# Stick-breaking triangle sums: one fp32 matmul against two fp32r matmuls on high part and remainder

## The chip, the cores and the metric

One core of a Trainium2 chip runs the whole layer as one program. The metric is the device time of one execution in microseconds; shown is the median of three runs, and beside it one execution that was profiled.

## What is computed

One layer of a streaming encoder on x of 256 x 2048 (float32): a SwiGLU block (hidden width 5632) with a layer norm, a mixer with two branches (mLSTM with 4 heads of 256, stick-breaking attention with 8 heads of 128) whose outputs are merged by sigmoid gates, a layer norm, a second SwiGLU block with a norm, and a gated addition of a small projection of p. What the change touches is the stick-breaking branch. Per head, for a block of 128 queries t and all keys s up to the block's end:

```
z = q k^T * scale
log_one_minus = where(s < t, log_sigmoid(-z), 0)
cum = cumsum(log_one_minus, axis=-1)
rem = cum[..., -1:] - cum
att = where(s < t, exp(log_sigmoid(z) + rem), 0)
out = att @ v
```

`rem` at key s is the sum of `log_one_minus` over the later keys. It is a sum along keys, and as keys lie on the partitions in the kernel, it is a matmul with a triangle of ones.

## The kernel before, in words

All large products run as three fp32r matmuls: both operands are split into a high part (converted to fp32r) and a remainder, and high x high, high x low and low x high are summed in PSUM (L1319, L1320, L1321). A weight tile of 256 x 512 arrives by DMA (L1238, queue of SP; some additions by GpSimd's queue, L372), ScalarE converts it to the high part (L1264), VectorE subtracts to get the remainder (L1268), and then it is used. Raw weights, split weights, activations and most other tiles share one pool of 51 pages; six smaller "temp" tiles of 128 x 512 hold intermediate values, and eight PSUM banks hold sums.

The order of the work is written out by hand. `program` is a list of units; a unit is six matmuls (two blocks of 128 rows, three matmuls each) of one weight tile for one half of the rows. Side work (norms, transposes, heads) is written as generators that say how long to wait before their next step. The scheduler `Sched` has a clock that moves by 6 x 0.2161 at each unit of 512 columns (L1322); after each unit, it runs every step that is due and then splits the weights that may be split (L1328, L1329):

```
        sched.now += 6 * 0.2161 * u.cols / COL
        ...
        sched.run()
        splits_due()
```

Each engine executes its own instructions in the order in which they are written here. `bank(delay)` looks for a place for the next step that is at least 3.0 away from other steps that take a PSUM bank (L84 to L91, L220).

`stick(h)` (L976 to L1017) is one head of the branch. It starts when its columns of q, k and v are there and at least 12.0 after the one before; three "lanes" take the eight heads in turn (L1043). Its steps: scores k q^T into PSUM (L984, three blocks of 128 x 128 side by side: 384 columns); z and |z| by ScalarE (L987, L988), exp and ln (L990, L991); after 6.5, the sum to sp = softplus(z) on VectorE (L993) and the mask of the two diagonal blocks (L866, called at L994); after 8.5 ("s1"), the triangle sums into one PSUM bank:

```
        nc.tensor.matmul(ps[:], tri[:], sp[:, n], start=True, stop=False)
        nc.tensor.matmul(ps[:, P:2 * P], ones[:], sp[:, 2 * P:3 * P], start=False, stop=True)
        nc.vector.tensor_tensor(out=z[:, n], in0=z[:, n], in1=ps[:], op=ALU.subtract)
```

The first (L997) has the triangle as stationary operand and 384 columns of sp moving, both float32; the second (L998) adds the whole later block to the earlier one's sums. Then VectorE subtracts from z (L999), ScalarE takes exp (L1002), the mask again (L1004), and the product with v (L1008) is split for the next projection (L1012, L1014). `tri` and `ones` are float32 constants; GpSimd makes the triangle from ones at the start (L278). The warming matmuls at the start are at L1198, called at L1200 and L1300. Lines of helpers: L243 is any activation of ScalarE, L239 a load of its table, L293 transposes of inputs, L295, L299 and L300 their conversion, copy and remainder, L420 and L592 sums of the seven-product scheme, L962, L969 and L970 the transposes and splits of the mLSTM heads.

Of the kernel before, what the change touches and what calls it, by code (L numbers as in the profile page):

```python
# [8 lines left out]
F32 = mybir.dt.float32  # L9
F32R = mybir.dt.float32r  # L10
ACT = mybir.ActivationFunctionType
ALU = mybir.AluOpType

P = 128
# [40 lines left out]
DELAY = {  # L55
    "alpha": 24.0, "away": 5.0, "sig": 5.0, "form": 18.0, "ln_turn": 3.6, "ln_step": 2.1, "gb": 14.0, "h": 8.0, "silu": 6.0, "late": 9.0, "last": 5.0, "rest": 1.2, "mt": 3.2,
    "sbt": 4.6, "g0": 3.0, "g1": 4.0, "g2": 12.0, "cv0": 1.0, "cv1": 5.0, "cv2": 1.3,
    "m0": 4.0, "m1": 4.0, "m2": 2.0, "m3": 4.6, "m4": 4.6, "sa": 1.4, "s0": 6.5, "s1": 8.5, "s2": 3.0, "s3": 5.0, "s4": 5.5,
}


# [127 lines left out]
def kernel(  # L189
# [6 lines left out]
    nc = tc.nc  # L196
    x, out = x[0], out[0]
# [3 lines left out]
    consts = ctx.enter_context(tc.tile_pool(name="consts", bufs=1))  # L201
# [10 lines left out]
    def temp():  # L212
        sched.until(lambda: temps[0] < TEMP_BUFS)
        temps[0] += 1
        return temp_pool.tile([P, COL], F32, name="temp", tag="temp")

    def drop(n=1):
        temps[0] -= n

    def bank(delay):  # L220
        return sched.slot(delay, BANK_GAP)

    def misc(shape):
        return ps_pool.tile(shape, F32, name="ms", tag="ps")
# [4 lines left out]
    def act_tile():  # L229
        return page_pool.tile([P, 2, 4, P], F32R, name="actT", tag="page")  # L230
# [10 lines left out]
    def activate(out, in_, func, **kw):  # L241
        use_table(func)
        nc.scalar.activation(out, in_, func, **kw)  # L243


    ones = consts.tile([P, P], F32, name="ones")
# [24 lines left out]
    def bring_back():  # L271
        for k in range(2):
            for t in range(TT):
                res[t, k] = big()
                nc.sync.dma_start(out=res[t, k][:], in_=away[t * P:(t + 1) * P, k * 1024:(k + 1) * 1024])

    tri = consts.tile([P, P], F32, name="tri")
    nc.gpsimd.affine_select(tri[:], ones[:], pattern=[[-1, P]], compare_op=ALU.is_ge,  # L278
                            fill=0.0, base=0, channel_multiplier=1)

    bound = consts.tile([P, 1 + P], F32, name="bound")
    nc.vector.memset(bound[:], 3.0e38)
# [420 lines left out]
    def wait(*names):  # L703
        while not all(f in flags for f in names):
            yield 0.6
# [154 lines left out]
    def diag(tl):  # L860
        return tl[:, 0:512].rearrange("q (a s) -> q a s", s=S)[:, :, 0:P]

    def causal(tl, strict):

        b = bound[:, 1 - strict:1 - strict + P].rearrange("q (a s) -> q a s", a=1).broadcast_to([P, 2, P])
        nc.vector.tensor_tensor(out=diag(tl), in0=diag(tl), in1=b, op=ALU.min)  # L866
# [109 lines left out]
    def stick(h):  # L976
        yield from wait(*[(n, t, h) for n in ("sq", "sk", "sv") for t in range(TT)])
        due = max(sched.now, st.get("stick", 0.0))
        st["stick"] = due + STICK_GAP
        yield bank(due - sched.now)  # L980
        q, k = st["sq", "T", h // 4][:, h % 4], st["sk", "T", h // 4][:, h % 4]
        ps = misc([P, 3 * P])
        for s in range(2):
            nc.tensor.matmul(ps[:, 256 * s:256 + P * s], k[:, s * P:(s + 1) * P], q[:, s * P:], start=True, stop=True)  # L984
        z, sp = temp(), temp()
        n = slice(0, 3 * P)
        activate(z[:, n], ps[:], ACT.Copy, scale=DS ** -0.5)  # L987
        activate(sp[:, n], ps[:], ACT.Abs, scale=DS ** -0.5)  # L988
        yield DELAY["sa"]
        activate(sp[:, n], sp[:, n], ACT.Exp, scale=-1.0)  # L990
        activate(sp[:, n], sp[:, n], ACT.Ln, bias=ones[:, 0:1])  # L991
        yield DELAY["s0"]
        nc.vector.scalar_tensor_tensor(out=sp[:, n], in0=z[:, n], scalar=0.0, in1=sp[:, n], op0=ALU.max, op1=ALU.add)  # L993
        causal(sp, 1)  # L994
        yield bank(DELAY["s1"])
        ps = misc([P, 3 * P])
        nc.tensor.matmul(ps[:], tri[:], sp[:, n], start=True, stop=False)  # L997
        nc.tensor.matmul(ps[:, P:2 * P], ones[:], sp[:, 2 * P:3 * P], start=False, stop=True)  # L998
        nc.vector.tensor_tensor(out=z[:, n], in0=z[:, n], in1=ps[:], op=ALU.subtract)  # L999
        drop()  # L1000
        yield DELAY["s2"]
        activate(z[:, n], z[:, n], ACT.Exp)  # L1002
        yield DELAY["s3"]
        causal(z, 1)  # L1004
        yield bank(DELAY["s4"])
        ps = misc([P, S])
        for s in range(2):
            nc.tensor.matmul(ps[:, P * s:], st["sv", s][:, h * DS:(h + 1) * DS], z[:, 256 * s:256 + P * s],  # L1008
                             start=(s == 0), stop=(s == 1))
        parts = [(ysbT.get(h // 4, t)[:, :, h % 4], ps[:, t * P:(t + 1) * P]) for t in range(TT)]  # L1010
        for dst, src in parts:
            nc.scalar.copy(dst[:, 0], src)  # L1012
        for dst, src in parts:
            nc.vector.tensor_tensor(out=dst[:, 1], in0=src, in1=dst[:, 0], op=ALU.subtract)  # L1014
        for t in range(TT):
            ysbT.mark(h // 4, t, 1)
        drop()  # L1017
# [25 lines left out]
    def lane():  # L1043

        for h in heads:
            yield from stick(h)
# [148 lines left out]
    def warm(n):  # L1195
        ps = misc([P, P])
        for _ in range(n):
            nc.tensor.matmul(ps[:], ones[:], ones[:], start=True, stop=True)  # L1198
# [56 lines left out]
    def split_one():  # L1255
        j = pos["split"]
        w = weights[j]
        make(j)
        assert w.made or not w.make
        r = w.raw.tile[:, :, :w.cols]  # L1260
        splits[j] = [page_pool.tile([P, 2, COL], F32R, name="split", tag="page") for _ in range(2)]
        hi, lo = (h[:, :, :w.cols] for h in splits[j])
        for ks in pieces(j):
            nc.scalar.copy(hi[:, ks], r[:, ks])  # L1264
            make(j + 1)
            if weights[min(j + 1, len(weights) - 1)].made or not weights[min(j + 1, len(weights) - 1)].make:
                make(j + 2)
            nc.vector.tensor_tensor(out=lo[:, ks], in0=r[:, ks], in1=hi[:, ks], op=ALU.subtract)  # L1268
        pos["split"] += 1
        for f in w.soon:  # L1270
            assert f.raw.tile is not None
            f.make()
            f.made = True
        pos["raw"] -= len(w.frees)
        for r in w.frees:
            r.tile = None
        loads()

    def splits_due():
        most = pos["at"] + 3 if pos["at"] < 8 else len(weights)  # L1280
        while pos["split"] < most and len(splits) < limits(pos["split"])[1]:
            split_one()
            if at_edge(pos["split"]):
                break
# [13 lines left out]
    sched.run()  # L1298
    splits_due()
    warm(WARM2)  # L1300
    for u in program:
        if isinstance(u, (Boundary, Mode)):
            continue
        if not isinstance(u, Unit):
            u()
            continue
        sched.until(lambda: u.act.ready(u.chunk, u.tt))
        j = u.tile.index
        pos["at"] = max(pos["at"], j)
        while pos["split"] <= j:  # L1310
            split_one()
        if u.start:
            u.acc["ps"] = ps_pool.tile([P, COL], F32, name="mm", tag="ps")
        ps = u.acc["ps"][:, :u.cols]
        a, w = u.act.tiles[u.chunk, u.tt], splits[j]
        for k in range(2):
            hi, lo = a[:, 0, u.sub + k], a[:, 1, u.sub + k]
            first, last = u.start and k == 0, u.stop and k == 1
            nc.tensor.matmul(ps, hi, w[0][:, k, :u.cols], start=first, stop=False, skip_group_check=u.onto)  # L1319
            nc.tensor.matmul(ps, hi, w[1][:, k, :u.cols], start=False, stop=False, skip_group_check=u.onto)  # L1320
            nc.tensor.matmul(ps, lo, w[0][:, k, :u.cols], start=False, stop=last, skip_group_check=u.onto)  # L1321
        sched.now += 6 * 0.2161 * u.cols / COL  # L1322
        u.tile.uses -= 1
        if u.tile.uses == 0:
            splits.pop(j)
        if u.stop:
            u.done(ps, u.tt)
        sched.run()  # L1328
        splits_due()  # L1329
# [27 lines left out]
```

## Time and profile before

| what | value |
|---|---|
| median of 3 runs | 2169.44 us (2167.12 to 2170.17) |
| the profiled execution | 2169.55 us |
| its span | 2167.7 us |
| TensorE busy (matmuls) | 2157.4 us, 9798 instructions |
| VectorE busy | 1893.7 us, 2088 instructions |
| ScalarE busy | 1347.1 us, 1658 instructions |
| L997, 16 instructions (two for each fp32 matmul) | first starts at 970.7, last at 1132.0 us |

The span goes from the first to the last instruction of the program in the profile; the execution's time has a little around it. In the rows of a timeline stand the start (us from the span's start), the duration, the engine, the line, the operation, the output and inputs, the shape, and how many instructions the row merges; in brackets the idle time of the engine before it and what ended that. In a table of groups, the numbers behind the bar are busy time in us, the mean duration of one in ns, and idle time before them. PE is TensorE, PEld its weight loads, DVE VectorE, ACT ScalarE, POOL GpSimd. In the table by stretches the numbers are the stretch, its length, busy time and instructions of each engine in that order, the granted clock, the share of the DMA engines, and GB/s.

### The profile page before, as it was taken

The numbers are of one execution on the slowest core, as the hardware profiler recorded it, in microseconds if no ns is written. First come the engines' busy times: TensorE is split into PE (matmuls) and PEld (weight loads), VectorE is DVE, ScalarE is ACT, GpSimd is POOL, SyncE is SP. The second block draws the span as 40 slices with busy tenths as digits, with TensorE's granted clock in tenths as the row PEclk, the third lists the DMA queues.
The fourth block names the chain that finished last, engine by engine and source line by source line (L and its number), as shares of the span: only waits on it lengthen the run. The fifth ranks groups of instructions, "written<-read, shape, count | busy, mean of one in ns | idle before, by whom it ended". The sixth has DMA issues, their size and how long they took to land.

```text
span 2167.7 us, 27662 instructions
## 1 busy us (share of the span) xinstructions
PE 2157.4 (100%) x9798; PEld 1783.9 (82%) x9798; DVE 1893.7 (87%) x2088; ACT 1347.1 (62%) x1658; POOL 218.2 (10%) x186
## 2 busy tenths in 40 slices
PE   9999999999999999999999999999999999999999
PEld 7888888888888888888888888888888888888887
DVE  6899999999998898887878975799999999999974
ACT  7656666656655765677866554556556656656572
POOL 0111111111100000101010000011111111111000
PEclk9999999999999999999999999999999999999999
DMA  9899899999994667978898976679989999999642
GB/s 349 215 275 270 249 270 275 272 280 268 266 318 140 215 218 219 242 218 203 260 272 260 273 260 203 201 192 279 267 245 276 279 266 277 257 276 294 237 166 87
DMA packets 283179, 535.98 MB, mean 247 GB/s; under 512 B 17144, under 2 KB 34464, under 8 KB 283040
## 3 DMA queue, kind: packets, MB, share of 16 engines
q1 hardware_dynamic: 234624, 440.87, 59.9%
q0 software_dynamic: 48416, 93.33, 23.9%
q8 instruction: 77, 1.26, 0.2%
q14 instruction: 62, 0.51, 0.1%
HBM read 527.85 MB, written 6.29 MB: 246 GB/s over the span
## 4 chain that ended last, share of the span: by engine, by line
PE 93%; issue 2%; DMA 2%; DVE 2%; ACT 0%; POOL 0%; SPq 0%; POOLq 0%; DVEq 0%; ACTq 0%
PE mm L1319 30%; PE mm L1321 30%; PE mm L1320 30%; DMA raw<-in_ffn_w_dram 2%; PE ms L293 1%; DVE split L1268 1%; PE ms L519 0%; DVE raw L366 0%; PE ms L984 0%; PE ms L906 0%; PE ms L921 0%; PE ms L997 0%; POOL raw L372 0%; PE ms L1008 0%; DMA actT<-ymaway 0%
## 5 line engine op out<-in xcount | busy, mean ns | idle before, releaser
L1264 ACT CAST split<-raw 128x1024 fp32r<-128x1024 f32 (+1 forms) x1089 | 1089.4, 1044 | 513.8 <-DMA raw<-in_ffn_w_dram 172.7
L1268 DVE TENSOR_TENSOR split<-raw,split 128x1024 fp32r<-128x1024 f32 (+1 forms) x1089 | 1277.8, 1212 | 141.5 <-ACT split L1264 134.6
L1319 PE MATMUL mm<-split,actT 128*128 128x512 f32 x3064 | 1203.0, 393 | 1.2 <-DVE big L420 1.2
L1321 PE MATMUL mm<-split,actT 128*128 128x512 f32 x3064 | 1189.5, 388 | 0.6 <-DVE actT L300 0.6
L1320 PE MATMUL mm<-split,actT 128*128 128x512 f32 x3064 | 1188.4, 388 | 1.0 <-DVE split L1268 1.0
L1321 PEld LDWEIGHTS mm<-split,actT 128*128 128x128 f32 x3064 | 575.8, 188 | 120.7 <-DVE actT L300 1.4
L1320 PEld LDWEIGHTS mm<-split,actT 128*128 128x128 f32 x3064 | 576.6, 188 | 115.9 <-DVE split L1268 3.4
L1319 PEld LDWEIGHTS mm<-split,actT 128*128 128x128 f32 x3064 | 576.3, 188 | 115.5 <-issue 2.6
L372 POOL DMA_DIRECT2D raw<-in_ffn_w_dram x140 | 169.7, 1441 | 1204.9 <-DVE split L1268 809.6
L366 DVE TENSOR_TENSOR raw<-raw 128x1024 f32<-128x1024 f32 x190 | 231.6, 1220 | 1.6
L372 POOL DMA_DIRECT2D raw<-in_w_in_dram x38 | 46.0, 1426 | 505.7 <-DVE split L1268 432.5
L295 ACT CAST actT<-ms 128x512 fp32r<-128x512 f32 x60 | 35.1, 586 | 77.7 <-PE ms L293 73.2
L644 DVE SCALAR_TENSOR_TENSOR big<-mm,big 128x512 f32<-128x512 f32 x112 | 76.5, 685 | 2.9 <-PE mm L1321 2.8
L592 DVE TENSOR_TENSOR temp<-mm,temp 128x512 f32<-128x512 f32 x108 | 73.1, 686 | 1.8 <-PE mm L1321 0.6
L300 DVE TENSOR_TENSOR actT<-ms,actT 128x512 fp32r<-128x512 f32 x60 | 41.1, 687 | 16.5 <-ACT big L299 11.0
L243 ACT ACTIVATE temp<-mm 128x512 f32<-128x512 f32 (+1 forms) x36 | 20.3, 570 | 49.5 <-PE mm L1321 49.5
L239 ACT ACT_TABLE_LOAD x34 | 43.6, 1283 | 0.6
L288 DVE TENSOR_TENSOR actT<-temp,actT 128x512 fp32r<-128x512 f32 x40 | 26.5, 689 | 17.3 <-ACT actT L287 17.2
L1180 DVE TENSOR_TENSOR temp<-temp,big 128x512 f32<-128x512 f32 (+1 forms) x10 | 5.8, 583 | 26.4 <-ACT temp L243 26.4
L287 ACT CAST actT<-temp 128x512 fp32r<-128x512 f32 x40 | 23.9, 620 | 8.0 <-DVE temp L311 7.4
L243 ACT ACTIVATE rstd<-mv,eps 128x1 f32<-128x1 f32 x6 | 1.8, 295 | 41.8 <-DVE mv L502 41.8
L1123 DVE SCALAR_TENSOR_TENSOR big<-big,mm 128x512 f32<-128x512 f32 x8 | 5.5, 686 | 25.3 <-PE mm L1321 25.3
(133 smaller groups left out, 605.6 us busy)
## 6 DMA issues: line engine op xcount, KB each, us to landing
raw<-in_ffn_w_dram SPq DMA_DIRECT2D x527, 512.0 KB, 6.9
raw<-in_w_in_dram SPq DMA_DIRECT2D x144, 512.0 KB, 5.3
raw<-in_ffn_w_dram POOLq DMA_DIRECT2D x140, 512.0 KB, 9.8
raw<-in_w_in_dram POOLq DMA_DIRECT2D x38, 512.0 KB, 9.0
raw<-in_w_out_dram SPq DMA_DIRECT2D x32, 512.0 KB, 5.5
raw<-in_w_ple_gate_dram SPq DMA_DIRECT2D x32, 512.0 KB, 5.2
raw<-in_w_in_dram SPq DMA_DIRECT2D x56, 256.0 KB, 3.8
raw<-in_w_up_m_dram SPq DMA_DIRECT2D x16, 512.0 KB, 6.8
```

Source lines behind the costliest of these rows:

```text
L239: nc.scalar.preload_act_table_set(table[0])
L295: nc.scalar.copy(dst[:, 0], ps[:])
L300: nc.vector.tensor_tensor(out=dst[:, 1], in0=ps[:], in1=dst[:, 0], op=ALU.subtract)
L366: nc.vector.tensor_tensor(out=out.tile[:, :, :cols], in0=a.tile[:, :, :cols], in1=b.tile[:, :, :cols], op=ALU.add)
L372: nc.gpsimd.dma_start(out=out.tile[:, :, :cols], in_=src, accum_op=ALU.add)
L592: nc.vector.tensor_tensor(out=out, in0=a, in1=b, op=op)
L644: nc.vector.scalar_tensor_tensor(out=xs, in0=ps, scalar=0.5, in1=xs, op0=ALU.mult, op1=ALU.add)
L1264: nc.scalar.copy(hi[:, ks], r[:, ks])
L1268: nc.vector.tensor_tensor(out=lo[:, ks], in0=r[:, ks], in1=hi[:, ks], op=ALU.subtract)
L1319: nc.tensor.matmul(ps, hi, w[0][:, k, :u.cols], start=first, stop=False, skip_group_check=u.onto)
L1320: nc.tensor.matmul(ps, hi, w[1][:, k, :u.cols], start=False, stop=False, skip_group_check=u.onto)
L1321: nc.tensor.matmul(ps, lo, w[0][:, k, :u.cols], start=False, stop=last, skip_group_check=u.onto)
```

## The change

The triangle becomes an fp32r constant: GpSimd writes it to a temp tile, and ScalarE converts it once behind the second warming. In each head, sp is split after its mask into a high part (ScalarE's conversion) and a remainder (VectorE's subtraction), both in one page; the triangle sums are two fp32r matmuls of 384 columns, one on each part. The matmul with `ones` stays float32. The wait "s1" of 8.5 becomes 4.0 ahead of the split and 4.5 behind it.

```
-    "m0": 4.0, ... "s0": 6.5, "s1": 8.5, "s2": 3.0, ...
+    "m0": 4.0, ... "s0": 6.5, "s1a": 4.0, "s1": 4.5, "s2": 3.0, ...
...
-    tri = consts.tile([P, P], F32, name="tri")
-    nc.gpsimd.affine_select(tri[:], ones[:], pattern=[[-1, P]], compare_op=ALU.is_ge,
+    tri = consts.tile([P, P], F32R, name="tri")
+    lower = temp()[:, 0:P]
+    nc.gpsimd.affine_select(lower, ones[:], pattern=[[-1, P]], compare_op=ALU.is_ge,
                             fill=0.0, base=0, channel_multiplier=1)
+
+    def make_tri():
+        nc.scalar.copy(tri[:], lower)
+        drop()
...
         causal(sp, 1)
+        yield DELAY["s1a"]
+        halves = act_tile()
+        hi, lo = (halves[:, k].rearrange("q a s -> q (a s)") for k in range(2))
+        nc.scalar.copy(hi[:, n], sp[:, n])
+        nc.vector.tensor_tensor(out=lo[:, n], in0=sp[:, n], in1=hi[:, n], op=ALU.subtract)
         yield bank(DELAY["s1"])
         ps = misc([P, 3 * P])
-        nc.tensor.matmul(ps[:], tri[:], sp[:, n], start=True, stop=False)
+        nc.tensor.matmul(ps[:], tri[:], hi[:, n], start=True, stop=False)
+        nc.tensor.matmul(ps[:], tri[:], lo[:, n], start=False, stop=False)
         nc.tensor.matmul(ps[:, P:2 * P], ones[:], sp[:, 2 * P:3 * P], start=False, stop=True)
...
     warm(WARM2)
+    make_tri()
     for u in program:
```

More of the change, by code (lines that the diff above doesn't have):

```diff
@@ L57 @@
     "sbt": 4.6, "g0": 3.0, "g1": 4.0, "g2": 12.0, "cv0": 1.0, "cv1": 5.0, "cv2": 1.3,
-    "m0": 4.0, "m1": 4.0, "m2": 2.0, "m3": 4.6, "m4": 4.6, "sa": 1.4, "s0": 6.5, "s1": 8.5, "s2": 3.0, "s3": 5.0, "s4": 5.5,
+    "m0": 4.0, "m1": 4.0, "m2": 2.0, "m3": 4.6, "m4": 4.6, "sa": 1.4, "s0": 6.5, "s1a": 4.0, "s1": 4.5, "s2": 3.0, "s3": 5.0, "s4": 5.5,
 }
```

## The prediction

> **What bounds the kernel now.** I read the page first: span, busy time, the groups, then the chain; after it the waits of TensorE alone, the table by stretches, and the timeline of the stage in which the changed lines stand.
>
> ```profile
> span 2167.7 us, 27662 instructions
> PE 2157.4 (100%) x9798; PEld 1783.9 (82%) x9798; DVE 1893.7 (87%) x2088; ACT 1347.1 (62%) x1658; POOL 218.2 (10%) x186
> PE 93%; issue 2%; DMA 2%; DVE 2%; ACT 0%; POOL 0%; SPq 0%; POOLq 0%; DVEq 0%; ACTq 0%
> ```
>
> ```profile
> PE mm L1319 <- DVE big L420: 1.2, 1, 1.2
> PE ms L1198 <- DVE ones L247: 1.1, 1, 1.1
> PE mm L1320 <- DVE split L1268: 1.0, 2, 0.7
> PE ms L293 <- DMA big<-in_x_dram: 0.9, 2, 0.7
> PE mm L1321 <- DVE actT L300: 0.6, 2, 0.3
> PE ms L984 <- DVE actT L1014: 0.4, 1, 0.4
> ```
>
> ```profile
> 955.00:1150.00 195.00, 194.64 (x936) 162.29 (x935) 155.99 (x204) 149.26 (x225) 19.39 (x16) 1.00 0.85 242
> ```
>
> TensorE is busy for 2157.4 of 2167.7 us and has 93% of the chain. Its own waits (second fence: us in total, times, longest) add up to 5.2 us in the whole run. In the stretch of 955 to 1150 us, which holds all eight heads of the stick-breaking branch, it is busy 194.64 of 195.00 us at a granted clock of 1.00; VectorE is busy 80% there, ScalarE 77%. So a microsecond that leaves TensorE's queue leaves the span, and one that VectorE or ScalarE gains is free until TensorE waits for it. A busy column alone would not prove that, because matmuls overlap; the starts do:
>
> ```profile
> 966.65 0.39 PE L1319 MATMUL mm<-split,actT 128*128 128x512 f32 x1
> ...
> 970.50 0.40 PE L1321 MATMUL mm<-split,actT 128*128 128x512 f32 x1
> 970.73 0.81 PE L997 MATMUL ms<-temp,tri 128*128 128x384 f32 x2
> 971.38 0.39 PE L998 MATMUL ms<-temp,ones 128*128 128x128 f32 x2
> 971.52 0.47 PE L1319 MATMUL mm<-split,actT 128*128 128x512 f32 x1
> 971.83 0.39 PE L1320 MATMUL mm<-split,actT 128*128 128x512 f32 x1
> ```
>
> ```profile
> 1035.81 0.28 PE L1320 MATMUL mm<-split,actT 128*128 128x256 f32 x1
> ...
> 1037.37 0.28 PE L1321 MATMUL mm<-split,actT 128*128 128x256 f32 x1
> ```
>
> The first fence: 18 fp32r matmuls of 512 columns start evenly between 966.65 and 970.50, so one takes a place of 3.85/17 = 0.226 us in the queue (its 0.39 us of duration overlaps the next). The fp32 triangle matmul is two instructions and takes 971.38 - 970.73 = 0.65 us. The next ones, L998 and what follows, run without a gap, so no change of type costs anything that shows. The second fence: 14 fp32r matmuls of 256 columns, (1037.37 - 1035.81)/13 = 0.120 us each.
>
> **What the change takes off TensorE.** Per head, one fp32 matmul of 384 columns (0.65 us) becomes two fp32r matmuls of 384 columns. No row has that shape; 512 columns take 0.226 and 256 take 0.120, so 384 lie between, and halfway is 0.173 (bounds 0.120 and 0.226). Two are 0.346; the saving is 0.30 us a head (0.20 to 0.41) and 2.4 us for eight heads (1.6 to 3.3). L998 stays fp32 and stays as it is.
>
> [...]
>
> **What it adds.** One conversion on ScalarE and one subtraction on VectorE per head, 128x384 each, a page for six microseconds, and once a conversion of the triangle.
>
> ```profile
> L1264 ACT CAST split<-raw 128x512 fp32r<-128x512 f32 x10 | 6.1, 628 | 0.5 <-PE mm L1320 0.5
> L969 ACT CAST actT<-big 128x128 fp32r<-128x128 f32 x16 | 3.6, 319 | 0.0
> L993 DVE SCALAR_TENSOR_TENSOR temp<-temp 128x384 f32<-128x384 f32 x8 | 4.4, 552 | 0.0
> ```
>
> ScalarE: between 0.319 (128 columns) and 0.628 (512), so about 0.52 us. VectorE: 0.55, as L993 at the same size. Eight of each are 4.2 and 4.4 us, in a stretch where ScalarE is idle for 46 us and VectorE for 39. That idle time hides them; uncovered, they cost what TensorE waits, which is the next part. L866 and L993 stay.
>
> **The new wait.** Before, L997 needed only sp. Now the first matmul needs the conversion, the second needs the subtraction, and the subtraction needs the conversion. While TensorE waits, every matmul behind it waits too. Where they stand in the queues follows from the code: time in the scheduler moves by one unit (six matmuls, 6 x 0.2161) and a step that is due runs at the next unit's end. The 8.5 of s1 is thus seven units; the new 4.0 is four and 4.5 is four again. So L997 comes one unit later than before, and the halves are put into the queues four units ahead of it, 24 x 0.226 = 5.4 us of TensorE. The question is how far VectorE runs behind. Two of the eight heads:
>
> ```profile
> 1122.45 0.55 DVE L993 SCALAR_TENSOR_TENSOR temp<-temp 128x384 f32<-128x384 f32 x1
> ...
> 1128.08 1.22 DVE L1268 TENSOR_TENSOR split<-raw,split 128x1024 fp32r<-128x1024 f32 x1 [2.03 <-ACT split L1264]
> ```
>
> ```profile
> 1131.71 0.81 PE L997 MATMUL ms<-temp,tri 128*128 128x384 f32 x2
> ```
>
> Head 7: four units behind L993 the subtraction stands after the split of 1128.08, ends at 1128.08 + 1.22 + 0.55 = 1129.85, and is needed at 1131.71 plus the unit of 1.36: more than 3 us to spare.
>
> ```profile
> 1072.47 1.12 ACT L243 ACTIVATE big<-ms,cw 128x128 f32<-128x128 f32 x4
> 1073.47 0.90 ACT L969 CAST actT<-big 128x128 fp32r<-128x128 f32 x4
> 1074.26 2.00 ACT L1264 CAST split<-raw 128x1024 fp32r<-128x1024 f32 x2
> ```
>
> ```profile
> 1066.36 0.55 DVE L993 SCALAR_TENSOR_TENSOR temp<-temp 128x384 f32<-128x384 f32 x1
> ...
> 1074.62 1.22 DVE L366 TENSOR_TENSOR raw<-raw 128x1024 f32<-128x1024 f32 x1
> 1075.76 2.36 DVE L1268 TENSOR_TENSOR split<-raw,split 128x1024 fp32r<-128x1024 f32 x2
> ```
>
> ```profile
> 1075.38 0.81 PE L997 MATMUL ms<-temp,tri 128*128 128x384 f32 x2
> ```
>
> Head 4: four activations and four conversions (L969) of an mLSTM head hold ScalarE; the new conversion stands between the two of 1074.26 and ends near 1075.7. The subtraction stands between the two of 1075.76 and ends near 1076.9 + 0.55 = 1077.5. By the code's order this head's matmul had already been moved to eight units by the spacing of PSUM banks and does not come later, so TensorE would need it at 1075.6 and wait 1.9 us. Going through the other six in the same way, one (head 1) is about even and five have time to spare. So the present positions give about 1.9 us in all. But every head's chain grows by one unit, and three lanes take heads in turn, so the later heads meet other work: the tight place may go or another may come. Nothing fixes the sign of that; the waits lie between 0 and some 8 us (one microsecond in every head). I take 1.0, half of what the present positions give, since the one tight place may move either way.
>
> The subtraction also holds up what is behind it on VectorE when its conversion is late: the splits, which TensorE needs only units later, and L999 of another head, which only its own chain needs. [...]
>
> **The start and the pages.** The triangle's conversion comes behind the first four splits on ScalarE, near 12.5 us.
>
> ```profile
> 12.50 0.58 ACT L295 CAST actT<-ms 128x512 fp32r<-128x512 f32 x1
> ...
> 16.96 1.05 ACT L1264 CAST split<-raw 128x1024 fp32r<-128x1024 f32 x1 [0.88 <-DMA raw<-in_ffn_w_dram]
> ```
>
> It takes 0.32 us as L969 does, and the idle 0.88 before 16.96 takes it up; uncovered 0.3. I count 0. Eight more tiles pass through the 51 pages, each held for some 6 us; a weight load that would have taken that page comes later by up to that.
>
> ```profile
> ACT split L1264 <- DMA raw<-in_ffn_w_dram: 172.7, 90, 4.1
> ```
>
> Over the whole run ScalarE's splits wait 172.7 us for weights, in 90 waits of at most 4.1 us, and TensorE's six rows above show that almost none of it reaches TensorE: splits are made several units ahead. I count 0 here too; uncovered, one such wait is 4.1 us.
>
> **The sum.** The profiled execution took 2169.55 us, 1.9 us more than its span of 2167.7, and lies 0.1 us over the median of the three runs, 2169.44. -2.4 (matmuls) + 1.0 (waits for the halves) + 0 (start) + 0 (pages) = -1.4: 2168.1 us against the execution, 2168.0 against the median. The three runs spread over 3 us, and I take 0.2%, 4.3 us, as what a measurement can tell from no change: faster is below 2165.1, slower above 2173.8.
>
> **Rivals.**
> - TensorE waits for the low half in most heads. For it: heads 4 and 1, and a chain that now hops ScalarE, VectorE, TensorE where VectorE is 80% busy. Against it: six of eight heads fit. The price is the wait per head times eight, less 2.4: it loses from 0.3 us a head, and is slower by over 0.2% from (4.3 + 2.4)/8 = 0.84. At 1.0 us: 2169.44 + 8.0 - 2.4 = 2175.0.
> - A page taken at the wrong moment delays a weight load past its lead, and one wait of 4.1 us reaches TensorE: 2168.0 + 4.1 = 2172.1. For it: the written order has nearly all 51 pages in use in this stretch. Against it: the waits for loads are absorbed everywhere else.
> - The change doesn't do what it says: an fp32r matmul of 384 columns takes as long as each of the fp32 matmul's two instructions, 0.65/2 = 0.325 us, and nothing is saved: 2169.44 + 1.0 = 2170.4. Against it: places at 256 and at 512 columns lie on both sides, below 0.23.
> - More is gained: the matmuls save the 3.3 us of the bound, and the moved order drops some of the 5.2 us of waits, 1.2 at L420 and 0.4 at L1014: 2169.4 - 3.3 - 1.6 = 2164.5. Nothing aims at those waits.
>
> **How the numbers follow.** Forecast, 2168.0, between 2165.8 and 2170.5: 62%. Halves late in most heads, around 2175: 16%, of which 11 over 2173.8. A page, 2172.1: 11%, of which 2 over. No saving, 2170.4: 6%. More gained, 2164.5: 5%, of which 4 below 2165.1. So faster 4%, slower 13%, the same 83%. The range runs from 2165.6 (just under the forecast's own) to 2173.0 (over the page's case, below most of the late halves) and leaves out about 4 in 100 below and 15 above.
>
> **What would show it.** The profile after should hold sixteen matmuls on the two lines in place of L997, in places of about 0.17 us; eight conversions near 0.52 and eight subtractions near 0.55; L998 as it was. TensorE's waits should hold a row for the subtraction's line of 0 to 2 us. A row of several us there, or one for a split behind a DMA, means the first or second rival; places of 0.32 mean the third. I am wrong in the main step if TensorE's busy time between 955 and 1150 us does not fall by about 2 us, or if its waits in that stretch grow by more than 3.

## Result and profile after

| | before | changed |
|---|---|---|
| median | 2168.32 us (2166.99 to 2170.91, 21 runs) | 2164.95 us (2163.52 to 2167.39, 21 runs) |
| the profiled execution | 2169.55 us, span 2167.7 | 2164.03 us, span 2162.3 |

The ratio is 0.9985, with a 95% interval from 0.9978 to 0.9991: 3.4 us less, between 2.0 and 4.8. That is within the 0.2% that was called the same. The forecast was 1.4 us less, and 2164.95 lies 0.65 us under the range. Part of that is the base: over 21 runs the kernel before has 2168.32, not the 2169.44 of three.

The changed kernel's page, first the span, then busy time, then the chain:

```profile
span 2162.3 us, 27685 instructions
PE 2153.1 (100%) x9798; PEld 1782.0 (82%) x9798; DVE 1897.6 (88%) x2096; ACT 1344.6 (62%) x1663; POOL 218.2 (10%) x186
PE 91%; DVE 4%; issue 3%; DMA 2%; ACT 0%; POOL 0%; SPq 0%; DVEq 0%; POOLq 0%; ACTq 0%
```

TensorE has as many instructions as before and 4.3 us less busy time; VectorE has eight more and 3.9 us more. Its own waits in the changed kernel (us in total, times, longest):

```profile
PE ms L1209 <- DVE ones L247: 1.1, 1, 1.1
PE mm L1331 <- DVE actT L1025: 0.9, 1, 0.9
PE ms L298 <- DMA big<-in_x_dram: 0.7, 1, 0.7
PE mm L1333 <- DVE actT L305: 0.6, 2, 0.3
PE mm L1332 <- DVE split L1279: 0.4, 1, 0.4
PE ms L298 <- DVE actT L305: 0.4, 1, 0.4
```

There is no row for L1007 or L1008, the two triangle matmuls: the halves are never late. The wait of 1.2 us on L420 is gone, and so is the 0.4 of L984; a new one of 0.9 us stands at L1331. The first head in the changed kernel's timeline:

```profile
971.31 0.34 PE L1007 MATMUL ms<-actT,tri 128*128 128x384 f32 x1
971.48 0.34 PE L1008 MATMUL ms<-actT,tri 128*128 128x384 f32 x1
971.66 0.38 PE L1009 MATMUL ms<-temp,ones 128*128 128x128 f32 x2
971.80 0.47 PE L1331 MATMUL mm<-split,actT 128*128 128x512 f32 x1
972.11 0.39 PE L1332 MATMUL mm<-split,actT 128*128 128x512 f32 x1
```

From 971.31 to 971.66 the pair takes 0.35 us in place of 0.644, 0.175 each; the fp32 matmul by ones (L1009) and the large ones behind it stand as far apart as before (0.45 us from 971.66 to 972.11, and from 971.38 to 971.83 before). All eight heads read 0.346 to 0.351, 2.80 us in all against 5.15 before: 2.35 us less. What was added, from the table of groups:

```profile
L1004 DVE TENSOR_TENSOR actT<-temp,actT 128x384 fp32r<-128x384 f32 x8 | 4.4, 551 | 0.3 <-ACT actT L1003 0.3
L1003 ACT CAST actT<-temp 128x384 fp32r<-128x384 f32 x8 | 4.1, 516 | 2.7 <-PE mm L1333 1.8 <-DMA ymaway<-actT 0.9
```

To place the gain, count the fp32r matmuls of the large products (9192 in each kernel, in the same order) and take the time between the starts of the 4001st and the 5001st. All heads lie between them; before, these are 944.48 and 1186.91 us. This is called the stage from here on.

| kernel | stage, us | against before | rest of the span |
|---|---|---|---|
| before | 242.43 | | 1925.3 |
| changed | 239.30 | -3.13 | 1923.0 |
| changed, second profile | 239.28 | -3.15 | 1923.9 |
| new order alone | 241.50 | -0.93 | 1924.7 |
| new order, halves unused | 241.51 | -0.92 | 1923.1 |
| new matmuls in the old order | 245.42 | +2.99 | 1926.1 |
| halves one unit ahead | 254.37 | +11.94 | 1924.4 |
| pair twice | 242.05 | -0.38 | 1923.8 |
| high part only | 237.83 | -4.60 | 1922.5 |
| ones on the halves | 239.21 | -3.22 | 1923.0 |
| 4.4 ahead of the product | 240.85 | -1.58 | 1922.0 |
| 4.4, halves a unit earlier | 239.19 | -3.24 | 1926.3 |

The stage repeats to some 0.02 us (changed and its second profile; new order with and without halves). The rest, in which all kernels do the same work but for one small conversion at the start, ranges over 4.3 us from profile to profile. So the difference of 5.4 us between the first two spans is not the change's: 3.13 us of it are the stage. Of the rest, about 1 us falls before the eighth large matmul, which starts at 10.44 us before and at 9.40 in the changed kernel; it also starts at 10.34 in the kernel with 4.4 and the halves a unit earlier, whose start is the changed kernel's, so that is not its work either. What differs there is how long the first large matmuls stand more than 0.3 us apart instead of 0.23: until 10.20 us before (rows at 8.93, 9.36, 9.78, 10.20, 10.44), only until 8.26 in the changed kernel (7.92, 8.26, 8.49, 8.72).

### The profile page after: what moved, and what is told of

Its sections match the earlier page's. It is cut to its first block, busy times and chain, and to the rows that moved or that the text cites. A ratio compares the mean times of both kernels' runs of the same rounds, so it can differ in the third digit from the quotient of the medians.

```text
span 2162.3 us, 27685 instructions
## 1 busy us (share of the span) xinstructions
PE 2153.1 (100%) x9798; PEld 1782.0 (82%) x9798; DVE 1897.6 (88%) x2096; ACT 1344.6 (62%) x1663; POOL 218.2 (10%) x186
## 4 chain that ended last, share of the span: by engine, by line
PE 91%; DVE 4%; issue 3%; DMA 2%; ACT 0%; POOL 0%; SPq 0%; DVEq 0%; POOLq 0%; ACTq 0%
PE mm L1331 29%; PE mm L1333 29%; PE mm L1332 29%; DMA raw<-in_ffn_w_dram 2%; DVE split L1279 2%; PE ms L298 1%; PE ms L524 0%; DVE actT L293 0%; POOL raw L377 0%; DVE raw L371 0%; PE ms L911 0%; PE ms L1019 0%; PE ms L989 0%; PE ms L926 0%; ACT split L1275 0%
## 5 line engine op out<-in xcount | busy, mean ns | idle before, releaser
L1331 PE MATMUL mm<-split,actT 128*128 128x512 f32 x3064 | 1201.2, 392 | 0.9 <-DVE actT L1025 0.9
L1331 PEld LDWEIGHTS mm<-split,actT 128*128 128x128 f32 x3064 | 575.7, 188 | 115.5 <-ACT big L243 1.1
L243 ACT ACTIVATE temp<-mm 128x512 f32<-128x512 f32 (+1 forms) x36 | 20.3, 569 | 49.9 <-PE mm L1333 49.9
L243 ACT ACTIVATE rstd<-mv,eps 128x1 f32<-128x1 f32 x6 | 1.8, 294 | 41.8 <-DVE mv L507 41.8
```

## Experiments

Theory A: 2.35 us come from the matmuls, about 0.65 from waits that the moved order of the stage drops and adds (1.23 and 0.36 gone, 0.94 new), the halves cost nothing. Rivals: M, the matmuls are all, and waits vary by chance; W, the added work or its wait costs something that the order gives back. All ratios are to the kernel before on the same chip, with 95% intervals.

**The order alone** (e1).

```
 (on the kernel before)
-"s1": 8.5
+"s1a": 4.0, "s1": 4.5
...
         causal(sp, 1)
+        yield DELAY["s1a"]
         yield bank(DELAY["s1"])
```

> The kernel before with only the changed waits: 4.0 and 4.5 in place of 8.5, nothing between them, the triangle sum still one fp32 matmul. The order of all work is that of the changed kernel, without its conversions, subtractions and fp32r matmuls. Theory A (the order carries part of the gain): TensorE's wait of 1.23 us near 1154 and of 0.36 near 1110 are gone, one of about 0.9 near 1007 is there, the time is 0.65 us under before (0 to 1.5). Rival M (matmuls alone): the waits differ from run to run and the time is that of before, within 0.3 us.

Measured: 0.9995 (0.9986 to 1.0003), medians 2166.35 and 2167.45. The medians alone do not decide it. The profile does. Two rows of before and one of this kernel's waits:

```profile
1152.09 0.39 PE L1321 MATMUL mm<-split,actT 128*128 128x512 f32 x1
1153.71 0.47 PE L1319 MATMUL mm<-split,actT 128*128 128x512 f32 x1 [1.23 <-DVE big L420]
```

```profile
PE mm L1320 <- DVE actT L1015: 0.9, 1, 0.9
```

The wait of 1.23 us on L420 is gone, and the 0.9 us on the last subtraction of a head (L1015 here, L1025 in the changed kernel) is there, as in the changed kernel, with the fp32 matmul still in place. So both waits follow the order of the work, not the matmuls, and they come back in each profile: M falls. The stage is 0.93 us shorter. By the idle time in brackets, 0.65 of it are the three waits. But that time counts from the end of the matmul before, 0.39 us behind its start, where the next could have started after 0.226. From start to start the wait of 1.23 us loses 1153.71 - 1152.09 - 0.226 = 1.39; in the same way that of 0.36 loses 0.52, and that of 0.94 loses 1.19. So 0.72 of the 0.93 are placed, and 0.2 are not.

**The halves made, and read by nothing** (e3): the edit above, and behind `yield DELAY["s1a"]` the four lines of the change that make `hi` and `lo`.

> As the kernel with only the changed order, and the conversion and subtraction are made in each head, but nothing reads them; the triangle sum stays one fp32 matmul. Theory A: idle time hides ScalarE's 4.1 us and VectorE's 4.4 us, so the time is that of the kernel with only the changed order, within 0.3 us. Rival W (the added work costs waits elsewhere): 1 to 4 us over that kernel, with waits of TensorE for VectorE's lines.

Measured: 0.9997 (0.9989 to 1.0006), medians 2167.01 and 2167.45; the stage is 241.51 us against 241.50. Eight conversions and eight subtractions cost TensorE nothing that a profile shows, and the page that they take does not either: W falls. The changed kernel has the same order and the same halves, so the stage gives the price of the matmuls alone: 241.51 - 239.30 = 2.21 us, a little less than the 2.35 between the starts of the pairs; the 0.14 are not placed.

**The new matmuls in the old order** (e2).

```
-"s1a": 4.0, "s1": 4.5
+"s1a": 4.0, "s1": 8.5
...
+        made = []
+        def parts_of():
             yield DELAY["s1a"]
             ...
+            made.append((hi, lo))
+        sched.spawn(parts_of())
         yield bank(DELAY["s1"])
+        hi, lo = made[0]
```

> The changed kernel with the order of before: the halves are written by a step of their own, four units after the sum of sp, and the triangle matmuls stand where the fp32 one stood, so that three units cover the halves (four in head 4). Theory A: 2.35 us less for the matmuls, the wait of 1.23 near 1154 is back, none near 1007, and the halves are late in one or two heads by 0 to 2 us: 0.5 to 2.4 us under before. The working on record says 1.9 us of wait in head 4 and some in head 1. Rival M: 2.4 under before, no wait for the halves.

Measured: 1.0007 (0.9998 to 1.0016), medians 2169.19 and 2167.45: not faster, where theory A gave 0.5 to 2.4 us less. TensorE's waits in this kernel (L1013 and L1014 are the pair, L1006 and L1007 the halves):

```profile
PE ms L1014 <- DVE actT L1007: 2.4, 3, 1.3
PE mm L1338 <- DVE split L1285: 2.4, 3, 1.4
PE mm L1337 <- DVE big L425: 1.2, 1, 1.2
...
PE ms L1013 <- ACT actT L1006: 0.3, 1, 0.3
```

The halves are late in three heads: 0.42 us in head 0 and 0.70 in head 1, where three units cover them, and 0.26 + 1.28 in head 4, where four do; the old wait of 1.2 us is back. (The 2.4 us on splits lie outside the stage.) Head 4 in the timeline, and the table by stretches there, where the granted clock is the third number from the end:

```profile
1078.82 0.44 PE L1013 MATMUL ms<-actT,tri 128*128 128x384 f32 x1 [0.26 <-ACT actT L1006]
1080.54 0.44 PE L1014 MATMUL ms<-actT,tri 128*128 128x384 f32 x1 [1.28 <-DVE actT L1007]
1080.82 0.59 PE L1015 MATMUL ms<-temp,ones 128*128 128x128 f32 x2
1081.06 0.78 PE L1337 MATMUL mm<-split,actT 128*128 128x512 f32 x1
1081.64 0.63 PE L1338 MATMUL mm<-split,actT 128*128 128x512 f32 x1
1082.06 0.63 PE L1339 MATMUL mm<-split,actT 128*128 128x512 f32 x1
```

```profile
1080.00:1081.00 1.00, 0.46 (x3) 0.46 (x4) 1.00 (x3) 1.00 (x3) 0.00 (x0) 0.93 1.02 274
1081.00:1082.00 1.00, 1.00 (x4) 0.87 (x4) 1.00 (x2) 0.97 (x3) 0.00 (x0) 0.50 1.14 264
1082.00:1083.00 1.00, 1.00 (x4) 0.74 (x3) 1.00 (x2) 1.00 (x2) 0.00 (x0) 0.50 1.10 236
1083.00:1084.00 1.00, 1.00 (x4) 0.81 (x3) 0.76 (x2) 0.85 (x2) 0.00 (x0) 0.50 1.10 262
1084.00:1086.00 2.00, 2.00 (x9) 1.60 (x9) 1.97 (x4) 1.27 (x2) 0.00 (x0) 0.93 1.07 335
```

The wait has a second price: behind it the clock is granted at 0.50, and a matmul of 512 columns takes 0.43 us in place of 0.226. Three rows hold 0.50 throughout; the two of 0.93 add 0.07/0.5 = 0.14 us and 2 x 0.14 = 0.28 us, so by this estimate it lasts 3.4 us, which at half the clock lose 1.7. From start to start, the four waits for the halves lose 0.58, 0.86, 0.41 and 1.54, together 3.4 us where their idle time is 2.7. That makes the account: -2.35 (pair) + 3.4 (waits for the halves) + 1.7 (clock) = +2.75, of the +2.99 that the stage shows; the rest is not placed.

**The halves one unit ahead** (e4).

```
-"s1a": 4.0, "s1": 4.5
+"s1a": 8.5, "s1": 0.9
```

> The changed kernel with the halves written one unit ahead of their matmuls (waits of 8.5 and 0.9 in place of 4.0 and 4.5). Theory A, with VectorE 2 to 5 us behind in this stage: TensorE waits 1 to 3 us for the low half in most heads, 8 to 24 us in all, less 2.4: 2174 to 2190 us, with the wait shown at the triangle's second line. Rival: the queue of TensorE and the lead of VectorE cover it anyway, and the time is that of the changed kernel, 2165.

Measured: 1.0064 (1.0051 to 1.0076), 2180.8 us, 13.4 over before, in theory A's range; 4.3 us of it are the clock, which the range had not counted. The waits, and the stretches behind that of head 0:

```profile
PE ms L1008 <- DVE actT L1004: 6.3, 4, 2.8
PE ms L1007 <- ACT actT L1003: 2.2, 2, 1.9
```

```profile
971.80:975.00 3.20, 0.44 (x1) 0.19 (x1) 3.13 (x8) 2.79 (x3) 2.44 (x2) 1.00 1.04 328
975.00:976.00 1.00, 0.92 (x4) 0.92 (x5) 1.00 (x2) 0.00 (x0) 0.00 (x0) 0.67 0.88 154
976.00:977.00 1.00, 1.00 (x3) 0.78 (x3) 1.00 (x3) 0.00 (x0) 0.00 (x0) 0.50 1.10 217
977.00:978.00 1.00, 1.00 (x4) 0.74 (x3) 1.00 (x2) 0.00 (x0) 0.00 (x0) 0.50 1.16 201
978.00:979.00 1.00, 1.00 (x4) 0.77 (x3) 1.00 (x2) 0.00 (x0) 0.00 (x0) 0.62 1.07 195
```

In four heads the low half is late, by 6.3 us in all, in two the high half, by 2.2. Behind head 0 the clock is halved for 3.4 us (0.33/0.5 + 2 + 0.38/0.5), and behind head 4, which waits 1.93 and 1.69 us, for 6.8. At half the clock the first loses 1.7 us; of the 6.8 us, 1.7 are waiting anyway, and the other 5.1 lose 2.6. So the wait that the change adds is real; what hides it are the units between the halves and the matmul. In the changed kernel four units or more cover the halves in every head. Against its stage, the old order, with three units in six heads and four in head 4, loses 6.1 us (0.9 of it the order), and this kernel loses 15.1: 9.7 of waits for the halves from start to start (8.5 of idle time), 4.3 of clock, and 0.7 of other waits that the moved order brings and takes; the rest is not placed. Only five heads have one unit here: the search for a bank leaves six in heads 1 and 3 and three in head 6, and none of those three waits.

**The pair issued twice** (e5).

```
+        nc.tensor.matmul(ps[:], tri[:], hi[:, n], start=True, stop=False)
+        nc.tensor.matmul(ps[:], tri[:], lo[:, n], start=False, stop=True)
         nc.tensor.matmul(ps[:], tri[:], hi[:, n], start=True, stop=False)
         nc.tensor.matmul(ps[:], tri[:], lo[:, n], start=False, stop=False)
```

> The changed kernel with the two fp32r triangle matmuls issued twice in each head (the first pair is thrown away by the second). Theory A: TensorE's queue maps one to one on the time, each matmul takes 0.175 us, so sixteen more cost 2.8 us over the changed kernel. Rival (TensorE has slack that its busy time hides): less than 1 us.

Measured: 1.0005 (0.9996 to 1.0014), medians 2168.4 and 2167.61. Against the changed kernel's 0.9985 that is 0.0020, or 4.3 us with an uncertainty of some 2.4 from the two intervals. The stage is sharper: 242.05 - 239.30 = 2.75 us for sixteen more matmuls, 0.172 each.

```profile
972.27 0.34 PE L1007 MATMUL ms<-actT,tri 128*128 128x384 f32 x1
972.44 0.34 PE L1008 MATMUL ms<-actT,tri 128*128 128x384 f32 x1
972.62 0.34 PE L1009 MATMUL ms<-actT,tri 128*128 128x384 f32 x1
972.79 0.34 PE L1010 MATMUL ms<-actT,tri 128*128 128x384 f32 x1
```

The four starts and that of L1011 at 972.97 stand 0.175 us apart: sixteen such places are 2.80 us, and they cost 2.75, one to one.

**The high part only** (e6): the second matmul of the pair is left out, so the sums lack the remainder.

> The changed kernel without the matmul on the remainder (the remainder is still written, the triangle sums lose it). Theory A: eight places of 0.175 us less, 1.4 us under the changed kernel, 4.4 to 4.8 under before. Rival (a share of the gain comes from the wait for the remainder being hidden by chance): the same 1.4 plus or minus new waits of more than 1 us.

Measured: 0.9982 (0.9973 to 0.9991), medians 2163.44 and 2167.61. The stage is 1.47 us under the changed kernel's for eight matmuls, 0.18 each; the waits are those of the changed kernel (the one near 1007 is 0.95). The same price from the other side.

**The matmul by ones on the halves too** (e7): `ones` is converted to fp32r once (its fp32 original moves to a temp tile, two columns of it to a constant), and L1009 becomes two fp32r matmuls of 128 columns, on `hi[:, 2 * P:3 * P]` and `lo[:, 2 * P:3 * P]`.

> The changed kernel with the matmul by ones as two fp32r matmuls of 128 columns on the same halves. If places go on falling with columns (0.226, 0.175, 0.120 at 512, 384, 256), 128 columns take about 0.067, the pair 0.13 in place of 0.227 us, and 0.7 us go in all. Rival: a short moving operand is slow in fp32r, each takes 0.11 us or more, and nothing or less than nothing is gained: up to 1.6 us over the changed kernel.

Measured: 0.9990 (0.9981 to 0.9998), medians 2164.54 and 2167.61; the stage is 239.21 against 239.30. The timeline of its first head:

```profile
971.59 0.22 PE L1014 MATMUL ms<-actT,onesr 128*128 128x128 f32 x1
971.65 0.27 PE L1015 MATMUL ms<-actT,onesr 128*128 128x128 f32 x1
971.76 0.44 PE L1337 MATMUL mm<-split,actT 128*128 128x512 f32 x1
972.04 0.39 PE L1338 MATMUL mm<-split,actT 128*128 128x512 f32 x1
```

From 971.59 to 972.04 there are 0.45 us, of which 0.226 belong to the large matmul: the pair takes 0.22, as the one in fp32 did (971.66 to 972.11 in the changed kernel). The rival was right: nothing is gained at 128 columns.

**Another order of the PSUM banks** (e8).

```
-"s4": 5.5
+"s4": 4.4
```

> The changed kernel with 4.4 in place of 5.5 ahead of the product with v: one unit less in most heads, so that the order of the PSUM banks differs near 1007. Theory A (waits of about a microsecond come and go with the order): the wait of 0.94 us near 1007 is gone or moved, and new ones may come where the mask is late for the product; the time differs from the changed kernel by -0.9 to +1.5 us. Rival: the wait at 1007 stays, nothing changes.

Measured: 0.9994 (0.9985 to 1.0002), medians 2165.96 and 2167.61. Its waits on the pair:

```profile
PE ms L1008 <- DVE actT L1004: 1.3, 1, 1.3
PE ms L1007 <- ACT actT L1003: 0.3, 1, 0.3
```

No wait near 1007 any more, but head 4 has moved a unit nearer to its halves (four units instead of five) and waits 0.25 + 1.28 us, the same as in the old order (there the clock was granted at 0.50 behind it, here it stayed at 1.00). The stage is 1.55 us longer than the changed kernel's, just over the top of what was expected.

The unit is not all that changed for head 4. ScalarE there, first in the changed kernel, then in this one:

```profile
1071.82 0.50 ACT L1003 CAST actT<-temp 128x384 fp32r<-128x384 f32 x1
1072.22 1.13 ACT L243 ACTIVATE big<-ms,cw 128x128 f32<-128x128 f32 x4
1073.23 0.90 ACT L974 CAST actT<-big 128x128 fp32r<-128x128 f32 x4
```

```profile
1070.92 0.91 ACT L974 CAST actT<-big 128x128 fp32r<-128x128 f32 x4
1071.71 1.06 ACT L1275 CAST split<-raw 128x1024 fp32r<-128x1024 f32 x1
1072.66 0.52 ACT L1003 CAST actT<-temp 128x384 fp32r<-128x384 f32 x1
```

In the changed kernel the conversion of head 4 (L1003) stands ahead of the activations and conversions of the mLSTM head (L243, L974); here, as in the old order, it stands behind them. So in the changed kernel the low half is done at 1072.91 us, 3.27 us before the matmul that reads it starts at 1076.18.

**That order, and the halves one unit earlier** (e9).

```
-"s1a": 4.0, "s1": 4.5, ... "s4": 5.5
+"s1a": 3.0, "s1": 5.5, ... "s4": 4.4
```

> The changed kernel with 4.4 ahead of the product with v, and the halves written one unit earlier (3.0 and 5.5 in place of 4.0 and 4.5). Theory A: the wait of 0.94 us near 1007 stays away as with the 4.4 alone, and the five units that now cover the halves take away the 1.53 us that head 4 waited there: about 1 us under the changed kernel, 4 us under before. Rival: the new order brings another wait of the same size, and the time is that of the changed kernel.

Measured: 0.9986 (0.9977 to 0.9995), medians 2164.09 and 2168.25. Neither the wait near 1007 nor one on the pair is left; these are the rows that are not at the start:

```profile
PE mm L1332 <- DVE split L1279: 2.0, 3, 1.4
...
PE ms L1019 <- ACT big L243: 0.3, 1, 0.3
```

The 2.0 us lie at 1936 to 2002 us, far behind the heads, where other profiles have 0 to 0.7. The stage is 239.19 us, 0.11 under the changed kernel's instead of the 0.94 that went: 0.34 and 0.13 us are new waits on products with v (0.50 and 0.29 from start to start, against 1.19 for the one that went), and the rest is not placed. That is the rival's answer rather than theory A's; a version better than the changed kernel by more than the measurement can tell was not found.

**The changed kernel again** (e10).

> The changed kernel once more, beside the others on the same chip. Theory A: 3.0 us under before (matmuls 2.35, waits 0.65), with the wait of 0.94 near 1007 and none for the halves in this profile too. Rival (the median's 3.4 was all real): 3.4 or more.

Measured: 0.9985 (0.9976 to 0.9994), medians 2164.9 and 2168.25: 3.35 us. The stage is 239.28 us, and its wait near 1007 is 0.94 us again. Whether the median's 3.4 holds 0.3 us more than the stage's 3.1 cannot be told, since the interval reaches from 2.0 to 4.8.

## Why the prediction was wrong

- **What bounds the kernel: right.** Sixteen more matmuls cost 2.75 us, eight fewer save 1.47.
- **The saving of 2.4 us: right.** The pair takes 0.351 (0.346 worked out), 2.35 us less in all by the starts and 2.21 by the stage. For each matmul of the pair 0.173 was worked out, and the trace has 0.175.
- **The added work at nothing, the start and the pages at nothing: right**, the work and the pages by the kernel whose halves nobody reads, the start by the first large matmuls, which come no later than before.
- **The waits for the halves, +1.0: this step failed.** They are 0. The reading of the queues was not the fault: left in its old place, head 4 waits 1.54 us where 1.9 was worked out, and with the 4.4 again 1.53. What failed is the use of the present positions: the sentence that head 4's matmul "does not come later", and the place of its conversion behind four activations and four conversions. In the code's order of the changed kernel the matmul does come one unit later (behind 4554 large matmuls instead of 4548), because the halves' own step is rounded up to whole units and the search for a PSUM place then begins from there. That unit is 1.36 us, less than the wait of 1.53; but the mLSTM head's steps have moved too, and the conversion now stands ahead of them. The two together turn the wait into 3.27 us to spare; no run has one without the other. Nor does every head move by one unit: head 1, about even in the working, comes three units later (4158 instead of 4140), and with the old place it waits 0.70 us. That the tight place might go was said, and priced at half; it went whole.
- **One of the signs was no test.** The main step was to be wrong if TensorE's busy time between 955 and 1150 us did not fall by about 2 us. It fell by 0.58, from 194.64 to 194.06, though the pairs save 2.35: the stretch is full before and after, and 943 matmuls stand in it instead of 936. Time saved in a full queue shows in a stretch that is fixed by its work, not by its start and end times. The other signs came as said: sixteen matmuls in places of 0.175 us, conversions of 0.516, subtractions of 0.551, and the matmul by ones as it was.
- **The moved order: put among the rivals at 5% with "nothing aims at those waits".** Nothing aimed at them, yet any change of a delay redraws them: here 1.23 and 0.36 us went and 0.94 came, and the stage got 0.93 us shorter by the order alone. The sum counted new waits of the moved order, and not the old ones, which were in the quoted rows.
- **The base.** Three runs gave 2169.44 and 21 gave 2168.32. Of the 3.05 us between forecast and result, 1.1 are this, 1.0 the halves, and 0.9 the order; none of the three alone would have put the result outside the range.
- **The rival of the late halves** was sized without the halved clock behind a wait. With one unit of cover in five heads the kernel came to 13.4 us over before, against the 5.6 that were given for it, and 4.3 of that are the clock.

## What to carry to other kernels

Where TensorE never rests, count what leaves its queue: here an fp32 matmul with a triangle of ones and zeros as stationary operand, so that only the moving one is split, took 0.644 us at 384 columns and 0.351 as two fp32r matmuls. The split, on engines with idle time left (between 955 and 1150 us of the changed kernel ScalarE is 77% busy and VectorE 84%), cost the stage nothing (241.51 us against 241.50 with halves that nobody reads), and the halves were waited for in no head of the changed kernel, where enough units of other work lie between them and their use. How many are enough depends on what else stands in those engines' queues: three were too few for heads 0 and 1 and enough for four others, four were too few for head 4 behind an mLSTM head and enough for every other head that had four. In a hand-written order, a delay that changes moves everything behind it: run the order alone, without the new arithmetic, before crediting the arithmetic with the time. Compare stages between the same instructions, because the rest of two spans can differ by more than the change.

## What the runs showed of the hardware

- A wait of TensorE can cost twice. Behind 0.26 and 1.28 us with one matmul between them (the old order, head 4), the granted clock was 0.50 for 3.4 us, and a matmul of 512 columns took 0.43 us in place of 0.226; with one unit of cover the clock fell for as long behind 0.30 and 2.84 us (head 0), and for 6.8 us behind 1.93 and 1.69 (head 4; the mean over this whole run is 0.997). After nearly the same 0.25 and 1.28 us in the kernel with 4.4 ahead of the product it stayed at 1.00 (as the mean over that run is), and so it did after a single wait of 1.55 us in head 5 of the kernel with one unit of cover. So 1.5 us of waiting were enough in one run and not in two other places; what decides it was not shown.
- A pair of fp32r matmuls is no faster than one fp32 matmul at 128 moving columns: 0.22 us for either. At 384 columns the pair takes 0.351 and the fp32 matmul 0.644. A single fp32r matmul takes 0.120 at 256 columns, 0.175 at 384 and 0.226 at 512.
- The idle time that a profile shows before a matmul is less than what the wait costs: 1.23 us of it cost 1.39 from start to start, 0.94 cost 1.19.
